# A four-layer decoder trunk on one core: weights split a whole unit at a time, the second keys' strip behind the first, and other room for the inverses

## The chip, the core and the metric

The kernel runs on one core of one Trainium2 chip. TensorE (PE) multiplies matrices, VectorE (DVE) and ScalarE (ACT) do elementwise work and read TensorE's results, GpSimd (POOL) does elementwise work too, and SyncE (SP) issues most of the transfers. The metric is the device time of the whole launch in microseconds; lower is better.

## The reference

Four pre-norm layers act on x, 256 positions of 1024 channels, float32: a pooling mixer, a gated delta net (GDN), a latent attention (MLA), and a pooling mixer again. Each mixer has one input projection, a SiLU gate and one output projection. In the GDN layer, which is where most of this case lies, 8 heads have keys and queries of 128 and values of 256 channels; positions go in chunks of 64:

```python
proj = h @ w_in                       # q, k, v, gate, b, a
qkv = jax.nn.silu(causal_depthwise_conv(qkv, conv_w))     # 4 taps
q, k = l2norm(q) * DK ** -0.5, l2norm(k)
L = where(strict, einsum('bhnid,bhnjd->bhnij', k_beta, k) * decay, 0)
sol = triangular_solve(eye + L, [v_beta, k_beta * exp(g)])
attn = where(causal, einsum('bhnid,bhnjd->bhnij', q, k) * decay, 0)
# then a scan over the chunks with state, w_out behind the gate
```

## The kernel before

**Weights.** Nearly all the work is projections whose weights come from DRAM once. `weights` (L97) loads a unit, two k-blocks of 128 rows by 512 columns (512 KB), by SP into `raw` (three buffers). Each float32 weight is split: ACT casts it into a high part `whi` (L117, fp32r), and DVE subtracts to get the low part `wlo` (L119); for k-blocks listed in `pool`, POOL does the subtraction in DVE's place. The high and low parts lie in the pool `ring`, nine tiles of 512 columns for each. TensorE then does three products in place of one: high by high, low by high and high by low. With `chan=True` (L127 to L129) the channels of the result lie on the partitions, 256 columns (all positions) a product; otherwise (`rows`, L168) positions lie on the partitions and a product has 512 columns. The run of products for one block of 512 output columns is called a strip.

**The GDN layer.** An order is written out by hand in a string of stages, one letter and number each: g a gate's strip, k and q keys and queries (four heads a strip), v a values' strip with its finish, d the decays, a the products `LT` of the keys with each other (`lower`), s the substitution, i the inverses, u the later products. The string before is

```python
order = "g0 k0 d a0 g1 k1 a1 s q0 v0 v1 v2 q1 V3 i c3 g2 u0 u1 g3".split()
```

It sets the order in which the program is written; a scheduler then interleaves the instructions of neighbouring stages on each engine from its own estimates, and decides which buffers share room.

**Around the triangular solve.** `channels` projects, convolves (L637, DVE; the first tap on ACT, L634), applies SiLU into `kqT` (ACT, L671), transposes on TensorE (`tp`, L677) and sums squares (`ssq`, L681). POOL takes the root (`rk`, L659). DVE scales the products of keys into `LT` (L694). `substitution` writes eight 32x32 blocks of `LT` to DRAM (`d_l`, L720, SP) and reads them back laid out by block (`Lb`, L723), then inverts all 64 blocks on POOL in 31 steps of two instructions (`pr`, L728, and `Tb`, L732). POOL sends `Tb` to DRAM (`d_t`, L735) and back into `T` (L739). POOL also multiplies `Gb` with the queries (L760). `inverses` transposes `T` into `U` (DVE, L811), and from the 32x32 inverses builds those of 64x64: `pairs` for both halves of the positions (TensorE, L820 and L826), then `whole` (L834, L838, L844). After them come `u` (L861) and the scan over the chunks (L888 to L914).

**Buffers.** `big` tiles are four KB a partition in a pool whose slots the scheduler hands out. `inverses` has two tiles `X1` of its own among them. The tile `kqT` of the second queries lies where `Lb` was.

## Time and profile before

| | us |
|---|---|
| median of 3 runs | 859.29 |
| lowest and highest run | 856.95, 861.53 |
| the profiled execution | 860.12 |
| its span | 858.3 |
| granted TensorE clock, mean over the span | 0.988 |

In the profile an engine is busy while it carries out instructions; the time that it stands idle is put down to what released it, written behind an arrow. A line number is that of the kernel before. The granted clock is the share of full TensorE speed (2.4 GHz) that the chip allowed; the lower level, 1.2 GHz, reads 0.5. The chain of waits follows the work that ended last back to the start.

### The profile page before, as it was taken

Reading aid. Unit: us, or ns where it says so; the run is one execution under the profiler, and the core shown is the slowest. Engines: PE = TensorE matmul, PEld = TensorE weight load, DVE = VectorE, ACT = ScalarE, POOL = GpSimd, SP = SyncE. Lnnn points to the kernel's source line nnn. Section 1 sums busy time; section 2 is a strip of 40 time slices with the busy share of each in tenths; the row PEclk is TensorE's granted clock in tenths of the full one; section 3 lists DMA queues with packets and bytes.
Section 4 is the critical chain, followed back from the end, with each engine's and each line's share of the span. In section 5 each row is a group of like instructions: output and inputs, shape, how many; then the busy total and the mean of one; then the engine's idle time right before and its main releaser. Section 6 shows DMA issues by size and latency. Waiting matters only on the chain.

```text
span 858.3 us, 16132 instructions
## 1 busy us (share of the span) xinstructions
PE 836.9 (98%) x5967; PEld 778.9 (91%) x5967; DVE 594.2 (69%) x1140; ACT 490.2 (57%) x1007; POOL 155.2 (18%) x295
## 2 busy tenths in 40 slices
PE   6999999999999989999999999999999999999996
PEld 5999998988999988788979998999989989999986
DVE  4689866556988976355577659678767668867852
ACT  5566564467855744355465654566555475555642
POOL 4000000233237980022212002000000210000012
PEclk8999999999999999899999999999999999999999
DMA  6766666646655554123547676743552546556551
GB/s 196 245 190 185 179 194 198 194 138 198 193 141 168 171 149 131 66 67 106 173 139 217 198 171 172 195 127 97 172 163 82 175 148 209 182 179 196 190 201 50
DMA packets 109239, 140.42 MB, mean 164 GB/s; under 512 B 21228, under 2 KB 51112, under 8 KB 109160
## 3 DMA queue, kind: packets, MB, share of 16 engines
q1 hardware_dynamic: 106800, 137.65, 53.1%
q0 software_dynamic: 528, 1.58, 0.7%
q8 instruction: 47, 0.77, 0.4%
q10 hardware_dynamic: 1832, 0.16, 0.2%
q14 instruction: 32, 0.26, 0.1%
HBM read 137.79 MB, written 1.58 MB: 162 GB/s over the span
## 4 chain that ended last, share of the span: by engine, by line
PE 82%; POOL 7%; DVE 5%; DMA 3%; issue 2%; ACT 1%; SPq 0%; POOLq 0%; ACTq 0%; DVEq 0%
PE acc L168 33%; PE acc L128 11%; PE acc L127 11%; PE acc L129 11%; POOL Tb L732 3%; POOL pr L728 2%; PE aux L127 2%; PE aux L128 2%; PE aux L129 2%; DVE wlo L119 1%; DMA gain<-in_norm_g_dram 1%; DVE cv L637 1%; DVE h L304 1%; PE aux L861 1%; DMA Gb<-d_g 1%
## 5 line engine op out<-in xcount | busy, mean ns | idle before, releaser
L119 DVE TENSOR_TENSOR wlo<-raw,whi 128x512 fp32r<-128x512 f32 (+1 forms) x493 | 342.5, 717 | 162.6 <-ACT whi L117 155.4
L117 ACT CAST whi<-raw 128x512 fp32r<-128x512 f32 (+1 forms) x508 | 301.8, 617 | 256.7 <-PE acc L168 100.4
L127 PE MATMUL acc<-hTh,whi 128*128 128x256 f32 x832 | 234.3, 282 | 1.2 <-DVE vc L637 1.2
L128 PE MATMUL acc<-hTl,whi 128*128 128x256 f32 x832 | 235.0, 283 | 0.0
L129 PE MATMUL acc<-hTh,wlo 128*128 128x256 f32 x832 | 233.8, 281 | 0.0
L127 PEld LDWEIGHTS acc<-hTh,whi 128*128 128x128 f32 x832 | 156.9, 189 | 1.8 <-DVE vc L637 1.4
L128 PEld LDWEIGHTS acc<-hTl,whi 128*128 128x128 f32 x832 | 156.9, 189 | 0.4
L129 PEld LDWEIGHTS acc<-hTh,wlo 128*128 128x128 f32 x832 | 156.8, 189 | 0.2
L168 PE MATMUL acc<-wlo,yTh 128*128 128x256 f32 (+1 forms) x384 | 116.5, 319 | 0.0
L168 PE MATMUL acc<-whi,yTh 128*128 128x256 f32 (+1 forms) x384 | 116.4, 323 | 0.0
L168 PE MATMUL acc<-whi,yTl 128*128 128x256 f32 (+1 forms) x384 | 92.7, 322 | 0.0
L168 PEld LDWEIGHTS acc<-wlo,yTh 128*128 128x128 f32 x384 | 72.1, 188 | 5.1
L168 PEld LDWEIGHTS acc<-whi,yTh 128*128 128x128 f32 x384 | 71.7, 188 | 5.2
L168 PEld LDWEIGHTS acc<-whi,yTl 128*128 128x128 f32 x384 | 63.2, 188 | 5.5
L292 POOL TENSOR_TENSOR hg<-x,gain 128x256 f32<-128x256 f32 x18 | 14.9, 834 | 259.1 <-DVE x L354 257.4
L168 PE MATMUL acc<-wlo,hTh 128*128 128x512 f32 (+1 forms) x144 | 56.3, 396 | 0.4 <-DVE wlo L119 0.2
L168 PE MATMUL acc<-whi,hTh 128*128 128x512 f32 (+1 forms) x144 | 55.6, 394 | 0.7 <-ACT hTh L196 0.7
L168 PE MATMUL acc<-whi,hTl 128*128 128x512 f32 (+1 forms) x144 | 45.7, 389 | 0.0
L435 POOL COPY win<-u 128x4 f32<-128x4 f32 x8 | 2.8, 355 | 177.2 <-ACT u L429 177.2
L168 PEld LDWEIGHTS acc<-whi,hTh 128*128 128x128 f32 x144 | 27.5, 191 | 6.8 <-ACT hTh L196 1.7
L168 PEld LDWEIGHTS acc<-wlo,hTh 128*128 128x128 f32 x144 | 27.3, 190 | 6.8 <-DVE wlo L119 1.7
L168 PEld LDWEIGHTS acc<-whi,hTl 128*128 128x128 f32 x144 | 26.8, 190 | 5.5
(339 smaller groups left out, 1444.5 us busy)
## 6 DMA issues: line engine op xcount, KB each, us to landing
raw<-in_pool_w_in_dram SPq DMA_DIRECT2D x60, 512.0 KB, 4.5
raw<-in_gdn_w_in_dram SPq DMA_DIRECT2D x48, 512.0 KB, 3.9
raw<-in_pool_w_out_dram SPq DMA_DIRECT2D x32, 512.0 KB, 4.2
raw<-in_mla_w_in_dram SPq DMA_DIRECT2D x24, 512.0 KB, 4.6
raw<-in_mla_w_uq_dram SPq DMA_DIRECT2D x36, 256.0 KB, 3.4
raw<-in_pool_w_grp_dram SPq DMA_DIRECT2D x16, 512.0 KB, 4.1
raw<-in_gdn_w_out_dram SPq DMA_DIRECT2D x16, 512.0 KB, 3.7
raw<-in_mla_w_ukv_dram SPq DMA_DIRECT2D x32, 256.0 KB, 3.3
```

Of the source, the lines that this page charges most:

```text
L117: a = nc.scalar.copy(hi, v)
L119: b = e.tensor_tensor(out=lo, in0=v, in1=hi.bitcast(F32), op=ALU.subtract)
L127: nc.tensor.matmul(o, lhsT=lhs[0], rhs=rhs[0], start=start, stop=False)
L128: nc.tensor.matmul(o, lhsT=lhs[0], rhs=rhs[1], start=False, stop=False)
L129: return nc.tensor.matmul(o, lhsT=lhs[1], rhs=rhs[0], start=False, stop=stop)
L168: nc.tensor.matmul(o, lhsT=act(k, t * P, P)[x], rhs=parts[j][z][:, sl], start=k == first and x == z == 0, stop=k == last and x == 1)
L292: nc.gpsimd.tensor_tensor(out=self.early[t, a], in0=xs[t][:, sl], in1=self.g[:, sl], op=ALU.mult)
L304: nc.vector.scalar_tensor_tensor(out=h[:, cut:], in0=xs[t][:, sl], scalar=r[:, 0:1], in1=self.g[:, sl], op0=ALU.mult, op1=ALU.mult)
L637: nc.vector.scalar_tensor_tensor(out=o[:, d:], in0=ps[:, :S - d], scalar=tp(3 - d, c), in1=o[:, d:], op0=ALU.mult, op1=ALU.add)
L728: nc.gpsimd.tensor_tensor(out=pv, op=ALU.mult, in0=Lb[:, r, r + 1:, None].to_broadcast([M * Q, n, c]), in1=Tb[:, r:r + 1, :c].to_broadcast ...
L732: mark["blocks"] = nc.gpsimd.tensor_tensor(out=tv, in0=tv, in1=pv, op=ALU.subtract).ins
L861: nc.tensor.matmul(ps[:, c], lhsT=U[0][:, h, :], rhs=vR[h // 2][:, 0, c * DV:(c + 1) * DV], start=True, stop=True)
```

## The change

Three things are changed. In `weights` ACT casts a whole unit, up to 1024 columns, in one instruction, and DVE subtracts a whole unit in one, unless POOL has a part of it (then each k-block has its own subtraction, as before). The ring holds five tiles of 1024 columns in place of nine of 512. Units of one k-block remain 512 wide, and the eight casts of units of 320 columns become four of 640. In all ACT's casts go from 508 to 258 and DVE's subtractions from 493 to 257; TensorE's, POOL's and SP's counts don't change.

In the string of stages the second keys (k1, a1) and the substitution (s) go ahead of the gate's strip g1. The inverses' tiles `X1` are not allocated any more: they are views of `Lb` and `Tb`, whose contents are no longer needed then. Lines move by one to six in the kernel after.

```diff
-    ring = ctx.enter_context(tc.tile_pool(name="ring", bufs=9))
+    ring = ctx.enter_context(tc.tile_pool(name="ring", bufs=5))
...
-        parts = []
-        for k in range(n):
-            v = raw[:, k * cols:(k + 1) * cols]
-            lo = ring.tile([P, CW], F32R, tag="wlo", name="wlo")[:, :cols]
-            hi = ring.tile([P, CW], F32R, tag="whi", name="whi")[:, :cols]
-            held = held_back["free"] <= 0
-            held_back["free"] -= 1
-            with later(*(held_back["after"] if held else ())):
-                a = nc.scalar.copy(hi, v)
+        lo = ring.tile([P, KU * CW], F32R, tag="wlo", name="wlo")
+        hi = ring.tile([P, KU * CW], F32R, tag="whi", name="whi")
+        held = held_back["free"] <= 0
+        held_back["free"] -= n
+        with later(*(held_back["after"] if held else ())):
+            a = nc.scalar.copy(hi[:, :m], raw[:, :m])
+
+            for k in range(n) if pool else (0,):
+                sl = slice(k * cols, (k + 1) * cols) if pool else slice(0, m)
                 e = nc.gpsimd if k in pool else nc.vector
-                b = e.tensor_tensor(out=lo, in0=v, in1=hi.bitcast(F32), op=ALU.subtract)
-            parts.append((hi, lo))
+                b = e.tensor_tensor(out=lo[:, sl], in0=raw[:, sl], in1=hi.bitcast(F32)[:, sl],
+                                    op=ALU.subtract)
+        parts = [tuple(x[:, k * cols:(k + 1) * cols] for x in (hi, lo)) for k in range(n)]
...
-        order = "g0 k0 d a0 g1 k1 a1 s q0 v0 v1 v2 q1 V3 i c3 g2 u0 u1 g3".split()
+        order = "g0 k0 d a0 k1 a1 s g1 q0 v0 v1 v2 q1 V3 i c3 g2 u0 u1 g3".split()
...
-        Tb = big("Tb", B, B)[:M * Q]
+        Tb_ = big("Tb", B, B)
+        Tb = Tb_[:M * Q]
+        free = []
...
-            Lb = big("Lb", B, B)[:M * Q]
+            Lb_ = big("Lb", B, B)
+            Lb = Lb_[:M * Q]
+            free.extend((Lb_, Tb_))
...
-            X1 = [big("X1", H, P) for _ in range(NT)]
+
+            X1 = [a.rearrange("p (h a) c -> p h (a c)", h=H) for a in free]
```

The change moves instructions on the engines. The first place is DVE between the second keys' root and their `LT` products; `s1` and `s2` are the scales that `LT` needs, `cv` the queries' convolution of q0. Before:

```order
294 L705 TENSOR_TENSOR s1_2526<-rk_2522,beta_2466 128x2x4
295 L741 RECIPROCAL rki_2523<-rk_2522 128x16
296 L742 TENSOR_TENSOR kds_2528<-rk_2522,DT_2496 128x8
297 L637 SCALAR_TENSOR_TENSOR cv_3260<-acc_3121,tap_648,cv_3260 128x254
298 L637 SCALAR_TENSOR_TENSOR cv_3272<-acc_3122,tap_648,cv_3272 128x255
299 L707 TENSOR_TENSOR s2_2527<-s1_2526,rk_2522 128x2x4
300 L119 TENSOR_TENSOR wlo_3504<-raw_3498,whi_3505 128x512
301 L637 SCALAR_TENSOR_TENSOR cv_3260<-acc_3121,tap_648,cv_3260 128x253
302 L637 SCALAR_TENSOR_TENSOR cv_3261<-acc_3121,tap_648,cv_3261 128x255
303 L637 SCALAR_TENSOR_TENSOR cv_3272<-acc_3122,tap_648,cv_3272 128x254
304 L694 SCALAR_TENSOR_TENSOR LT_2530<-aux_3017,s2_2527,DT_2496 128x128 x4
305 L694 SCALAR_TENSOR_TENSOR LT_2531<-aux_3026,s2_2527,DT_2497 128x128 x4
```

and after:

```order
226 L119 TENSOR_TENSOR wlo_3139<-raw_3137,whi_3140 128x512
227 L708 TENSOR_TENSOR s1_2304<-rk_2300,beta_2244 128x2x4
228 L746 RECIPROCAL rki_2301<-rk_2300 128x16
229 L747 TENSOR_TENSOR kds_2306<-rk_2300,DT_2274 128x8
230 L710 TENSOR_TENSOR s2_2305<-s1_2304,rk_2300 128x2x4
231 L697 SCALAR_TENSOR_TENSOR LT_2308<-aux_2674,s2_2305,DT_2274 128x128 x4
232 L697 SCALAR_TENSOR_TENSOR LT_2309<-aux_2683,s2_2305,DT_2275 128x128 x4
233 L638 SCALAR_TENSOR_TENSOR cv_2979<-acc_2856,tap_616,cv_2979 128x255
234 L119 TENSOR_TENSOR wlo_3207<-raw_3205,whi_3208 128x1024
```

The convolution of q0 now stands behind `LT`, and one split stands ahead of it.

The second place is DVE behind the last convolution of the second queries (`cv`); `ssq` is their norm, `attnT` their products with the keys, and `U<-T` the transposes that need the inverted blocks back from DRAM. Before:

```order
399 L681 TENSOR_REDUCE ssq_2521<-sq_4010 128x2x2
400 L119 TENSOR_TENSOR wlo_4379<-raw_4373,whi_4380 128x512
401 L119 TENSOR_TENSOR wlo_4397<-raw_4395,whi_4398 128x512
402 L694 SCALAR_TENSOR_TENSOR attnT_3119<-aux_4021,rk_2522,DT_2496 128x128 x4
403 L694 SCALAR_TENSOR_TENSOR attnT_3120<-aux_4030,rk_2522,DT_2497 128x128 x3
404 L681 TENSOR_REDUCE ssq_2521<-sq_4018 128x2x2
405 L694 SCALAR_TENSOR_TENSOR attnT_3120<-aux_4030,rk_2522,DT_2497 128x128
406 L811 STREAM_TRANSPOSE U_4182<-T_2517 128x1024
407 L811 STREAM_TRANSPOSE U_4183<-T_2517 128x1024
```

and after:

```order
315 L119 TENSOR_TENSOR wlo_4009<-raw_4007,whi_4010 128x1024
316 L638 SCALAR_TENSOR_TENSOR cv_3653<-acc_3518,tap_616,cv_3653 128x253
317 L817 STREAM_TRANSPOSE U_3825<-T_2295 128x1024
318 L817 STREAM_TRANSPOSE U_3826<-T_2295 128x1024
319 L684 TENSOR_REDUCE ssq_2299<-sq_3669 128x2x2
320 L119 TENSOR_TENSOR wlo_4027<-raw_4025,whi_4028 128x512
321 L697 SCALAR_TENSOR_TENSOR attnT_2854<-aux_3680,rk_2300,DT_2274 128x128 x4
322 L697 SCALAR_TENSOR_TENSOR attnT_2855<-aux_3689,rk_2300,DT_2275 128x128 x3
323 L684 TENSOR_REDUCE ssq_2299<-sq_3677 128x2x2
324 L697 SCALAR_TENSOR_TENSOR attnT_2855<-aux_3689,rk_2300,DT_2275 128x128
```

The transposes have moved ahead of the norms and the `attnT` products.

The third place is TensorE at the end of the last values' strip (`acc` from `hTh1`, 256 columns) and the first products of the inverses (`aux<-T,LT`); the products of 512 columns are the gate's strip g2. Before, with 13 products of g2 ahead of the inverses' first, of which the last seven are shown:

```order
2130 L168 MATMUL acc_4328<-whi_4332,hTh0_2258 128x512
2131 L168 MATMUL acc_4328<-wlo_4331,hTh0_2258 128x512
2132 L168 MATMUL acc_4328<-whi_4336,hTh0_2258 128x512
2133 L168 MATMUL acc_4328<-wlo_4335,hTh0_2258 128x512
2134 L168 MATMUL acc_4328<-whi_4332,hTl0_2259 128x512
2135 L168 MATMUL acc_4328<-whi_4336,hTl0_2259 128x512
2136 L168 MATMUL acc_4327<-whi_4354,hTh0_2258 128x512
2137 L820 MATMUL aux_4190<-T_2517,LT_2530 128x64 x8
```

and after:

```order
2047 L128 MATMUL acc_3704<-hTh1_2059,whi_3798 128x256
2048 L129 MATMUL acc_3704<-hTl1_2060,whi_3798 128x256
2049 L130 MATMUL acc_3704<-hTh1_2059,wlo_3797 128x256
2050 L826 MATMUL aux_3831<-T_2295,LT_2308 128x64 x8
2051 L169 MATMUL acc_3968<-whi_3973,hTh0_2050 128x512
2052 L169 MATMUL acc_3968<-wlo_3972,hTh0_2050 128x512
```

No product of g2 stands ahead of the inverses' first now.

The order on SP changes at one place: the eight `d_l` transfers, in a row before, go as six, a weight load, and two; between them and `Lb` one weight load stands in both kernels. The tile of the second queries (`kqT`) lies in the room of the first queries' tile after the change, and no longer in that of `Lb`. On POOL a memset and a split that stood between the send of `Tb` and the loads of `T` stand behind the loads.

## Rows read from the trace of the kernel before

**Rows 1.** The page: busy time (share) and instructions by engine; the chain's shares.

```profile
PE 836.9 (98%) x5967; PEld 778.9 (91%) x5967; DVE 594.2 (69%) x1140; ACT 490.2 (57%) x1007; POOL 155.2 (18%) x295
...
PE 82%; POOL 7%; DVE 5%; DMA 3%; issue 2%; ACT 1%; SPq 0%; POOLq 0%; ACTq 0%; DVEq 0%
```

**Rows 2.** Stretches: length, busy time (instructions) by engine, clock, DMA share, GB/s.

```profile
270.00:300.00 30.00, 27.73 (x233) 27.11 (x231) 30.00 (x53) 20.04 (x42) 27.34 (x35) 1.00 0.56 169
300.00:330.00 30.00, 27.59 (x187) 25.21 (x185) 24.93 (x48) 14.13 (x29) 18.70 (x31) 0.94 0.51 144
330.00:360.00 30.00, 28.55 (x175) 23.78 (x175) 11.27 (x18) 11.61 (x23) 1.30 (x1) 0.89 0.32 108
690.00:720.00 30.00, 29.60 (x203) 26.77 (x202) 20.17 (x32) 20.31 (x37) 2.41 (x6) 1.00 0.61 193
```

**Rows 3.** Groups by line and shape: count, busy, mean ns, idle before and its releasers.

```profile
L119 DVE TENSOR_TENSOR wlo<-raw,whi 128x512 fp32r<-128x512 f32 x485 | 338.8, 721 | 160.5 <-ACT whi L117 153.2 <-PE acc L129 2.0 <-PE aux L128 1.5
L117 ACT CAST whi<-raw 128x512 fp32r<-128x512 f32 x500 | 298.3, 620 | 253.9 <-PE acc L168 98.8 <-PE acc L128 79.6 <-DMA raw<-in_pool_w_in_dram 21.1
...
L168 PE MATMUL acc<-wlo,hTh 128*128 128x512 f32 x128 | 51.5, 407 | 0.4 <-DVE wlo L119 0.2
...
L447 DVE TENSOR_TENSOR pl<-p,ph 128x1024 fp32r<-128x1024 f32 x8 | 9.7, 1218 | 0.9 <-ACT ph L446 0.7
...
L446 ACT CAST ph<-p 128x1024 fp32r<-128x1024 f32 x8 | 8.4, 1048 | 1.1 <-DVE p L444 1.1
```

**Rows 4.** The same groups, from 261 to 306 us alone.

```profile
L119 DVE TENSOR_TENSOR wlo<-raw,whi 128x512 fp32r<-128x512 f32 x24 | 22.0, 927 | 2.0 <-PE acc L129 2.0
...
L117 ACT CAST whi<-raw 128x512 fp32r<-128x512 f32 x25 | 14.9, 623 | 9.6 <-DMA raw<-in_gdn_w_in_dram 8.6 <-PE acc L129 0.8 <-PE acc L128 0.2
```

**Rows 5.** Timeline of SP's queue: start, length, line, transfer, count.

```profile
250.69 3.99 SPq L720 DMA_DIRECT2D d_l<-LT  x8
254.78 0.40 SPq L104 DMA_DIRECT2D raw<-in_gdn_w_in_dram  x1
255.93 0.51 SPq L723 DMA_DIRECT2D Lb<-d_l  x1
```

**Rows 6.** Timeline of DVE around the second keys' products.

```profile
245.78 0.85 DVE L637 SCALAR_TENSOR_TENSOR cv<-acc,tap,cv 128x254 f32<-128x254 f32 x2
246.55 1.30 DVE L707 TENSOR_TENSOR s<-s,rk 128x8 f32<-128x8 f32 x1
...
249.55 2.15 DVE L694 SCALAR_TENSOR_TENSOR LT<-aux,s,DT 128x128 f32<-128x128 f32 x8
```

**Rows 7.** Timeline of POOL, the substitution's first and last step and what follows.

```profile
260.95 0.23 POOL L728 TENSOR_TENSOR pr<-Lb,Tb 64x31 f32<-64x31 f32 x1 [13.12 <-DMA Lb<-d_l]
...
305.33 0.25 POOL L732 TENSOR_TENSOR Tb<-Tb,pr 64x31 f32<-64x31 f32 x1
305.54 1.27 POOL L760 TENSOR_TENSOR Gb<-Gb,kqT 128x512 f32<-128x512 f32 x1
```

**Rows 8.** Timeline of ACT, first silu of the second queries; idle before, releaser in brackets.

```profile
305.29 0.42 ACT L671 ACTIVATE kqT<-cv 128x256 f32<-128x256 f32 x1 [3.46 <-POOL pr L728]
```

**Rows 9.** Timeline of TensorE: waits in the layer, and two products of 512 columns.

```profile
277.89 0.65 PE L788 MATMUL tp<-ident,vc 128*128 128x128 f32 x4 [1.11 <-ACT vc L784]
...
305.76 0.69 PE L677 MATMUL tp<-ident,kqT 128*128 128x128 f32 x2 [2.41 <-ACT kqT L671]
...
316.85 0.40 PE L168 MATMUL acc<-wlo,hTh 128*128 128x512 f32 x1
317.08 0.39 PE L168 MATMUL acc<-whi,hTh 128*128 128x512 f32 x1
...
352.91 1.83 PE L844 MATMUL aux<-U,X 64*64 64x64 f32 x16 [0.79 <-DVE X L841]
```

**Rows 10.** Timeline of DVE, products of queries and keys, transposes of the inverted blocks.

```profile
314.10 1.89 DVE L694 SCALAR_TENSOR_TENSOR attnT<-aux,rk,DT 128x128 f32<-128x128 f32 x7
...
318.75 2.37 DVE L811 STREAM_TRANSPOSE U<-T 128x1024 f32<-128x1024 f32 x2 [1.91 <-DMA T<-d_t]
```

## The prediction

> **What bounds the kernel now.** I read the busy times and the chain of waits first. TensorE is busy for 836.9 of 858.3 us and carries 82% of the chain, POOL 7% and DVE 5% [rows 1]. The split of the weights is ACT's and DVE's largest work (298.3 and 338.8 us [rows 3]), but neither engine is the bound over the whole. So the edit is worth what TensorE stands still for, or runs slowly for, and this is read by stretches [rows 2]: nearly full elsewhere (29.60 of 30 us at 690:720, a layer's border), TensorE loses 2.3 us at 270:300, 2.4 at 300:330 and 1.4 at 330:360. There the granted clock falls too, to 0.94 and 0.89: 0.06 x 30 = 1.8 and 0.11 x 30 = 3.3 us of full-clock time, the lower level being 0.5 (1.2 of 2.4 GHz). All three stretches are the gated-delta layer. About 11 us in sum is all that can be had there; the remaining idle time (start, end, borders) is not touched.
>
> Then I read who is waited for. At 270:300 DVE is busy for the whole 30 us: its 24 splits beside POOL's substitution take 927 ns, against 721 over the kernel [rows 3, 4], and TensorE's 1.11 us wait at 277.89 ends with the values' silu behind them. At 300:330 the substitution is the bound. It runs on POOL from 260.95 to 305.58, 44.6 us with hardly a gap [rows 7]; ACT's first silu of the second queries waits 3.46 us for its last `pr`, and TensorE 2.41 us for that silu [rows 8, 9]. What starts it is the DMA of `Lb`, issued at 255.93 behind `d_l` at 250.69 and `LT` at 249.55 [rows 5, 6]. At 330:360 the inverses come with little to put between their dependent steps, and the clock falls before L861.
>
> **The split, a unit at a time.** A unit of 1024 columns cost ACT 2 x 620 = 1240 ns and DVE 2 x 721 = 1442 ns. The same widths as single instructions stand in the trace: ACT's cast of `ph` 1048 ns, DVE's `pl` 1218 ns [rows 3]. So 246 pairs save ACT 0.19 us each, 47 us; 232 pairs save DVE 0.22 us each, 52 us. Elsewhere TensorE is full, so this counts nothing: its cover is TensorE's own strip. It counts at 270:300. About 12 units fall beside the substitution, 12 x 0.22 = 2.7 us off DVE, 12 x (2 x 0.927 - 1.218) = 7.6 us if the collision with POOL cost an instruction and not its columns. I take the lower end, since TensorE's 2.3 us of idle time there is the most that can be gained, and DVE and the raw weights (ACT waited 8.6 us for them [rows 4]) share it. Taken: 1.5 us, bounds 0 and 2.3, and it is lost again if TensorE merely reaches the wait for the second queries sooner.
>
> Against it stands latency: the first half of a unit was ready after 0.620 + 0.721 = 1.34 us, now after 1.048 + 1.218 = 2.27 us, 0.93 later. Five units of look-ahead hide it inside a strip; at the start and three borders the cover is the work ahead of the first strip. Zero taken, bounds 0 and 4 x 0.93 = 3.7 us.
>
> A rule speaks against this edit. The Trainium skill ("Perfetto Trace Analysis", section "Optimizing Scalar/DVE Operations") says that grouping pays where the engine is saturated, but that with unsaturated Scalar or Vector engines that cause bubbles elsewhere "breaking up instructions may allow work to be completed sooner". The trace agrees with the first half at 270:300 alone, where DVE is full; for the rest of the kernel the page's rule is my last rival.
>
> **The second keys' strip behind the first.** On TensorE the gate's strip g1 was ahead of it: 48 matmuls of 512 columns. Such matmuls follow each other by 317.08 - 316.85 = 0.23 us [rows 9], so 11 us. The strip of k1 ends that much sooner. Its transposes do not: in the new order they stand inside g1's strip, and DVE must first finish the decay tiles, the first keys' norm and its own splits. Following the new DVE queue with the durations of before, `LT` of the second keys ends at about 245 to 246, not 251.7. The order shows why: the pieces of q0's convolution and one split that stood between the norm and `LT` are gone, five of the pieces and the split between 245.78 and 249.55 (a piece is 0.85 / 2 = 0.42 us [rows 6]), 2.8 us with the split's 0.7. `d_l`'s eight DMAs now go as 6 and 2 with a weight load between, moving `Lb` by 0.4 us at most (one such issue is 0.40 [rows 5]). So the substitution starts and ends about 6 us sooner, 299.5 instead of 305.5 [rows 7]; bounds 3 (only these pieces gone) and 10 (no new DVE queue in the way).
>
> **What waits for it, and what is new.** Before, the wait of TensorE at 305.76 was 2.4 us [rows 9]. (1) The second queries' tile now lies where POOL's `Gb<-Gb,kqT` reads the first's, so the silu waits for that too: 1.27 us behind the substitution [rows 7]. (2) On POOL a memset and a split between `d_t` and the load of `T` are behind it; by the durations that remain `T` lands some 12 us behind the substitution, 13.2 before (318.75 - 305.54 [rows 7, 10]). (3) On DVE the transposes `U<-T` now stand ahead of the two norms, a split and the `attnT` products. Until `T` lands, DVE does nothing; behind it are 2.37 us of transposes, a norm of about 0.7, a split of 0.7 [rows 3] and the products, 1.89 / 7 = 0.27 us each [rows 10]. TensorE's next strip (g2) needs the bank of the first four: 12 + 2.4 + 0.7 + 0.7 + 4 x 0.27 = 16.9 us behind the substitution. TensorE is there about 2.5 us sooner by the work that is left to it, and stalls so long. Before, 13 matmuls of g2 stood ahead of L820; now none does. (4) Against time from the substitution's end, the second pair's products come at +28.8, before +29.8, but with 15 matmuls of 512 columns less behind TensorE: 15 x 0.23 = 3.5 us. So the net gain is the 6 us, plus 1.0, minus 3.5, minus up to 1.2 us of slow clock behind the stall: 6 - 2.7 = 3.3 at best and 6 - 3.9 = 2.1 at worst. I take 2.7. The 1.5 us of the split are inside it: TensorE's order carries them to the same wait.
>
> **The inverses' own room.** The tiles `Lb` and `Tb` are free by then: no copy, no wait, POOL's memsets move. It removes a slot, nothing on the path. What it lets the order do is put 6 matmuls (1.4 us) between L844 and the products before it; they cover one of the two waits of about 0.8 us that stand before 352.91 [rows 9]. Whether the clock then stays up before L861 is unknown from this trace: it gives 0, or up to 3.3 us [rows 2]. I take 0.5 for the covered wait and 0.8 for the clock, nearer to nothing since one wait of 0.79 remains.
>
> **Sum.** 860.1 (profiled execution) - 2.7 - 0.5 - 0.8 = 856.1, about 4.0 less; the median of the runs is 0.8 below that execution, so 855.3; I say 855.5.
>
> **Rivals.** *Full gain*: the substitution ends 9 to 10 us sooner, the silu and `T` are there when TensorE arrives, and the clock stays up to 360: 10 - 2.7 + 0.5 + 3.3 = 11, 848 us. For it: the strip itself is 11 us earlier. Against: DVE's queue, and TensorE's order that keeps the transposes late. *Hidden anyway*: the chain moves by about 3, new waits take 2.7 to 3.9, the clock falls as before: 859. For it: TensorE is full everywhere else and (1) and (3) are in the order for certain. *DVE stuck behind `T`* (the slower side): the substitution moves by less than 2.7 us, because the second keys' norm waits on DVE behind first keys' work. At an advance of 0, 2.7 to 3.9 us are lost, and a stall of over 4 us takes the clock down for another 1 to 2 us: 863 to 866, say 864.5. It decides below 2.7 us. For it: three waits are now in one chain. Against: q0's pieces are gone for certain. *Breaking up*: whole units make TensorE wait 0.93 us at the start and borders: 855.5 + 3.7 = 859, or 864 if the middle gives little. For it: TensorE idles at these places already; against: its waits for `wlo` in a strip come to 0.4 us in the whole kernel [rows 3].
>
> **How the numbers follow.** Forecast 0.40 (852 to 859), full gain 0.23, hidden 0.20, DVE stuck 0.12, breaking up 0.05. A measurement of this kernel tells about 0.5% from no change, 4.3 us: below 855.0, and above 863.6. Faster: 0.23 and just under half of the forecast, 0.42. Slower: most of DVE stuck and half of breaking up, with some for what I don't see: 0.16. Same: 0.42. The range goes from the full gain, 847.5, to the slower side, 863.5; about 1 in 10 is left out at each end.
>
> **What would show it.** In the new trace: casts near 1048 and 1218 ns; `LT` of the second keys ends near 245.5 and the first `pr` starts near 255; the last `Tb` near 299.5; a silu wait named after `Gb`, not `pr`; `U<-T` with a wait of several us; a stall of TensorE near 316; a clock at 330:360 above 0.89 or not. The forecast is wrong if the substitution's start moves by under 3 or over 9 us, if the splits slow TensorE at borders, or if the clock behind L861 goes another way.

## The result and the profile after

The kernel after takes 863.24 us (median; 861.29 to 865.92), the kernel before 859.70 in the same sessions: ratio 1.0039, 95% interval 1.0025 to 1.0053. It is slower, where about 4 us less were forecast. The profiled execution took 861.29 us, its span 859.5.

The page of after, busy times and the chain's shares, which answer to [rows 1]:

```profile
PE 834.2 (97%) x5967; PEld 780.0 (91%) x5967; DVE 568.4 (66%) x904; ACT 458.0 (53%) x757; POOL 168.5 (20%) x295
...
PE 76%; POOL 7%; DMA 5%; DVE 5%; issue 3%; ACT 2%; SPq 0%; POOLq 0%; ACTq 0%; DVEq 0%
```

DVE and ACT are busy for 26 and 32 us less. TensorE's share of the chain falls from 82 to 76% with the same number of instructions. Stretches of after, columns as in [rows 2]:

```profile
270.00:300.00 30.00, 30.00 (x255) 30.00 (x254) 26.33 (x43) 20.04 (x37) 27.57 (x32) 1.00 0.60 175
300.00:330.00 30.00, 22.75 (x152) 21.09 (x152) 16.30 (x32) 10.16 (x16) 18.26 (x33) 0.83 0.32 90
330.00:360.00 30.00, 28.76 (x183) 23.91 (x183) 13.49 (x17) 11.88 (x18) 1.77 (x1) 0.95 0.48 158
690.00:720.00 30.00, 28.43 (x193) 25.68 (x192) 18.06 (x21) 19.64 (x29) 3.27 (x7) 1.00 0.55 172
```

TensorE's idle time at 270:300 is gone, 2.3 us. At 300:330 it is idle for 7.25 us instead of 2.4, and the clock there is 0.83 instead of 0.94. The splits, over the whole kernel ([rows 3]) and beside the substitution ([rows 4]):

```profile
L119 DVE TENSOR_TENSOR wlo<-raw,whi 128x1024 fp32r<-128x1024 f32 x232 | 290.3, 1255 | 173.4 <-ACT whi L114 172.2
L114 ACT CAST whi<-raw 128x1024 fp32r<-128x1024 f32 x246 | 257.5, 1050 | 236.5 <-PE acc L169 94.0 <-PE acc L129 67.0 <-DMA raw<-in_pool_w_in_dram 26.3
```

```profile
L119 DVE TENSOR_TENSOR wlo<-raw,whi 128x1024 fp32r<-128x1024 f32 x13 | 18.4, 1416 | 2.5 <-ACT whi L114 2.5
```

SP's queue, DVE and POOL, as in [rows 5], [rows 6], [rows 10] and [rows 7]:

```profile
246.62 3.93 SPq L723 DMA_DIRECT2D d_l<-LT  x6
250.65 0.40 SPq L104 DMA_DIRECT2D raw<-in_gdn_w_in_dram  x1
251.09 0.96 SPq L723 DMA_DIRECT2D d_l<-LT  x2
252.15 0.40 SPq L104 DMA_DIRECT2D raw<-in_gdn_w_in_dram  x1
255.35 0.51 SPq L728 DMA_DIRECT2D Lb<-d_l  x1
```

```profile
245.47 2.16 DVE L697 SCALAR_TENSOR_TENSOR LT<-aux,s,DT 128x128 f32<-128x128 f32 x8
...
317.18 2.37 DVE L817 STREAM_TRANSPOSE U<-T 128x1024 f32<-128x1024 f32 x2 [5.02 <-DMA T<-d_t]
```

```profile
258.81 0.23 POOL L733 TENSOR_TENSOR pr<-Lb,Tb 64x31 f32<-64x31 f32 x1 [11.47 <-DMA Lb<-d_l]
...
268.39 1.43 POOL L733 TENSOR_TENSOR pr<-Lb,Tb 64x207 f32<-64x207 f32 x1
269.89 0.60 POOL L737 TENSOR_TENSOR Tb<-Tb,pr 64x207 f32<-64x207 f32 x1
...
305.76 0.24 POOL L737 TENSOR_TENSOR Tb<-Tb,pr 64x31 f32<-64x31 f32 x1
305.97 1.26 POOL L765 TENSOR_TENSOR Gb<-Gb,kqT 128x512 f32<-128x512 f32 x1
```

`LT` of the second keys is done at 247.6, 4.1 us sooner. Nearly all of that is won behind their norm, which comes only 0.4 us sooner: DVE ends its sums of squares (`ssq`) at 241.24, before at 241.68; it starts the scales that `LT` needs 1.6 us sooner. Before, then after:

```profile
241.00 0.68 DVE L681 TENSOR_REDUCE ssq<-sq 128x4 f32<-128x512 f32 x1
245.52 0.15 DVE L705 TENSOR_TENSOR s<-rk,beta 128x8 f32<-128x8 f32 x1
```

```profile
240.57 0.67 DVE L684 TENSOR_REDUCE ssq<-sq 128x4 f32<-128x512 f32 x1
243.92 1.26 DVE L708 TENSOR_TENSOR s<-rk,beta 128x8 f32<-128x8 f32 x1 [1.57 <-POOL rk L662]
```

`Lb` is issued only 0.6 us sooner: the eight `d_l` take 5.4 us to issue instead of 4.0, and `Lb` waits 3.3 us behind the last one (before 1.25). The first `pr` starts 2.1 us sooner (3.5 us behind the issue of `Lb`, before 5.0). But the step of 64x207 at 268.39 takes 1.43 us, its partner 0.60, and the substitution takes 305.76 + 0.24 - 258.81 = 47.2 us instead of 44.6. It ends at 306.0, 0.4 us later than before. ACT and TensorE then read (as [rows 8, 9]):

```profile
307.26 0.42 ACT L674 ACTIVATE kqT<-cv 128x256 f32<-128x256 f32 x1 [10.28 <-POOL Gb L765]
```

```profile
307.73 0.69 PE L680 MATMUL tp<-ident,kqT 128*128 128x128 f32 x2 [7.25 <-ACT kqT L674]
...
355.87 1.14 PE L850 MATMUL aux<-U,X 64*64 64x64 f32 x16 [1.24 <-DVE X L847]
```

TensorE has been waiting since 300.5: it came 3 us sooner, and the silu came 2 us later, 1.26 of them for `Gb`.

By layers, from the start of DVE's last update of x in one layer to that in the next, in us (the first layer's from the start; "again" is a second profile of the same kernel):

| kernel | pooling | GDN | MLA | pooling |
|---|---|---|---|---|
| before | 175.6 | 255.4 | 259.2 | 161.6 |
| before, again | 174.4 | 254.4 | 259.2 | 161.6 |
| after | 174.3 | 257.7 | 258.9 | 161.9 |
| after, again | 174.9 | 258.4 | 258.9 | 161.9 |
| after, borders in halves | 173.1 | 257.2 | 258.4 | 160.8 |
| after, no low parts beside the substitution | 173.7 | 246.8 | 258.8 | 161.8 |
| before, new string alone | 174.6 | 257.6 | 259.3 | 161.7 |

The first column moves by a microsecond between executions of one kernel. What the change adds stands in the GDN layer, 2.3 to 4.0 us; MLA gains 0.3 and the last layer loses 0.3 (by POOL's part of x, which ends later, MLA loses 0.7 and the last layer gains 0.4: the two together stay the same).

### The profile page after: what moved, and what is told of

The parts are those of the page before. It is cut to its first block, busy times and chain, and to the rows that moved or that the text cites. A ratio compares the mean times of both kernels' runs of the same rounds, so it can differ in the third digit from the quotient of the medians.

```text
span 859.5 us, 15387 instructions
## 1 busy us (share of the span) xinstructions
PE 834.2 (97%) x5967; PEld 780.0 (91%) x5967; DVE 568.4 (66%) x904; ACT 458.0 (53%) x757; POOL 168.5 (20%) x295
## 4 chain that ended last, share of the span: by engine, by line
PE 76%; POOL 7%; DMA 5%; DVE 5%; issue 3%; ACT 2%; SPq 0%; POOLq 0%; ACTq 0%; DVEq 0%
PE acc L169 32%; PE acc L130 10%; PE acc L129 10%; PE acc L128 10%; DMA raw<-in_pool_w_in_dram 3%; POOL pr L733 3%; POOL Tb L737 2%; PE aux L128 2%; PE aux L129 2%; PE aux L130 2%; DVE wlo L119 2%; ACT whi L114 1%; DMA raw<-in_mla_w_out_dram 1%; DVE cv L638 1%; PE aux L867 1%
## 5 line engine op out<-in xcount | busy, mean ns | idle before, releaser
L119 DVE TENSOR_TENSOR wlo<-raw,whi 128x1024 fp32r<-128x1024 f32 (+1 forms) x257 | 309.2, 1207 | 191.8 <-ACT whi L114 190.2
L114 ACT CAST whi<-raw 128x1024 fp32r<-128x1024 f32 (+2 forms) x258 | 265.3, 1032 | 245.8 <-PE acc L169 95.0
L129 PEld LDWEIGHTS acc<-hTl,whi 128*128 128x128 f32 x832 | 158.7, 191 | 0.3
L128 PEld LDWEIGHTS acc<-hTh,whi 128*128 128x128 f32 x832 | 158.7, 191 | 0.4
L130 PEld LDWEIGHTS acc<-hTh,wlo 128*128 128x128 f32 x832 | 158.6, 191 | 0.1
L293 POOL TENSOR_TENSOR hg<-x,gain 128x256 f32<-128x256 f32 x18 | 14.7, 829 | 257.1 <-DVE x L355 254.2
L169 PE MATMUL acc<-whi,hTl 128*128 128x512 f32 (+1 forms) x144 | 45.3, 388 | 0.1
L436 POOL COPY win<-u 128x4 f32<-128x4 f32 x8 | 6.1, 765 | 171.8 <-ACT u L430 171.8
```

The costliest lines, as they stand in the source:

```text
L114: a = nc.scalar.copy(hi[:, :m], raw[:, :m])
L119: b = e.tensor_tensor(out=lo[:, sl], in0=raw[:, sl], in1=hi.bitcast(F32)[:, sl], op=ALU.subtract)
L128: nc.tensor.matmul(o, lhsT=lhs[0], rhs=rhs[0], start=start, stop=False)
L129: nc.tensor.matmul(o, lhsT=lhs[0], rhs=rhs[1], start=False, stop=False)
L130: return nc.tensor.matmul(o, lhsT=lhs[1], rhs=rhs[0], start=False, stop=stop)
L169: nc.tensor.matmul(o, lhsT=act(k, t * P, P)[x], rhs=parts[j][z][:, sl], start=k == first and x == z == 0, stop=k == last and x == 1)
```

## The experiments

**The change again, and its parts one by one.** First the same kernel, for a second profile.

> The kernel after once more, for a second profile beside the same kernel before. Theory 1 (three causes in one chain: the transfers d_l land in 3.7 us instead of 1.9, POOL's substitution lasts 47.2 us beside splits of 1024 columns instead of 44.6, and the second queries' silu waits 1.27 us more): LT of the second keys ends about 4 us sooner than before (251.7), the first pr starts only 2 us sooner (about 258.8), the last Tb ends about 306, TensorE waits about 7 us for the silu; the ratio stays near 1.004. Theory 2 (the profile taken first was an accident of the transfers): the first pr starts by 256 or the substitution lasts under 45.5 us here.

Measured 862.26 us, ratio 1.0030 (1.0015 to 1.0046). First `pr` at 260.08, substitution 47.1 us, TensorE's wait 7.8 us. The first start is a microsecond later than expected, as is the whole execution; the rest repeats.

```diff
-    ring = ... bufs=9        # splits of 512 columns
+    ring = ... bufs=5        # weights() of the kernel after, old string, own X1
```

> Before with the splits by whole units and five ring tiles, and nothing else. Theory 1: the substitution lasts 46.5 to 47.5 us (before 44.6), each of its long steps beside a 1024-column split takes up to 1.4 us; the borders of layers lose 1 to 1.5 us each against before, the start gains 1; the time is 861 to 864 us. Theory 2 (the split is neutral and the order carries the loss): substitution 44.5 to 45.5 us, 857 to 860 us.

870.8 us, ratio 1.0123 (1.0092 to 1.0153): worse than either theory. The substitution is only 45.3 us long here, with 9 whole splits beside it, and 9 of its steps are held up. Most of the loss is ahead of it: `LT` ends at 260.2, 8.5 us later than before, though TensorE waits for only 2.8 us in the layer until then; the scheduler's order is another one. Later TensorE waits for the values' convolution and silu:

```profile
PE acc L128 <- DVE vc L638: 4.7, 1, 4.7
PE tp L789 <- ACT vc L785: 2.0, 1, 2.0
```

With the new string and the room as well, a kernel with the same splits is 7 us faster.

```diff
-        order = "g0 k0 d a0 g1 k1 a1 s q0 ...
+        order = "g0 k0 d a0 k1 a1 s g1 q0 ...
```

> Before with the new string of stages and nothing else; splits of 512 columns. The silu of the second queries waits for Gb here too. Theory 1: LT of the second keys ends 4 us sooner, d_l lands later than before (over 2.5 us, before 1.9) because weight loads run beside it, the first pr starts 2 to 3 us sooner, the substitution lasts 44 to 45.5 us, and the time is 856 to 860 us. Theory 2 (the order carries the loss): 862 to 865 us, with a wait of TensorE of over 5 us before the second queries' transposes.

860.5 us, ratio 1.0012 (0.9995 to 1.0029): no change that can be told. `LT` ends at 249.1, but `Lb` is issued at 256.8 and the substitution runs from 260.7 to 306.7. The sooner strip is lost before it reaches POOL. TensorE waits 7.6 us for the silu, as in after, the sign of theory 2, and yet the time is near theory 1's: this wait by itself doesn't make the kernel as slow as after. The substitution is 1.4 us longer than before with the same 24 halves beside it: 6 of its steps are held up by over 0.4 us (before none), 3 of them by 1.0 us, where two halves stand in a row on DVE.

```diff
-            X1 = [big("X1", H, P) for _ in range(NT)]
+            X1 = [a.rearrange("p (h a) c -> p h (a c)", h=H) for a in free]
```

> Before with the inverses in the room of Lb and Tb, and nothing else. The second queries' tile has a room of its own here, so its silu waits for nothing on POOL. Theory 1: the wait of 3.46 us on ACT and of 2.41 us on TensorE at 303 to 306 us is gone, but TensorE then reaches the inverses' first product before T has landed (about 13 us behind the substitution) and gives 1 to 2 us back there: 857 to 859 us. Theory 2 (room counts for nothing): within 0.5 us of before.

863.32 us, ratio 1.0041 (1.0024 to 1.0057), both theories missed. The silu waits for nothing on POOL, as expected, and TensorE runs into the next link:

```profile
PE aux L824 <- DMA T<-d_t: 4.4, 1, 4.4
PE acc L127 <- DVE vc L637: 1.2, 1, 1.2
PE tp L792 <- ACT vc L788: 1.1, 1, 1.1
PE acc L127 <- ACT gsg L557: 1.0, 1, 1.0
```

The wait at the silu, 2.4 us, is traded for one of 4.4 at `T`, and the granted clock at 300:330 is 0.83 here, before 0.94. Giving up two tiles changed the places of others; by the ratios the three parts cost 10.6, 1.0 and 3.5 us and together 3.4, so they don't add up (1.0 is within the spread).

**The wait for the tile.**

```diff
-            dst.append(big("kqT", 4, S))
+            dst.append(own[0] if which and hf else big("kqT", 4, S))   # a const tile
```

> After, with a room of its own for the second queries' tile (one memset more on POOL, long before); the order on every engine is that of after. Theory 1 (the chain from the keys over the substitution to the inverted blocks sets the end, and the wait for the tile only shows where TensorE meets it): the silu no longer waits on POOL, TensorE's stall of 7 us before the second queries' transposes goes, but TensorE then stands at the inverses' first product until T has landed, about 11 us behind the substitution, for 5 us or more; the time falls by 0 to 2 us against after. Theory 2 (the wait for the tile is the loss): the time falls by 5 us or more, to 857 us or below.

862.89 us, ratio 1.0044 (1.0026 to 1.0062), as after. The silu runs at 296.8, TensorE's transposes at 299.6, and then:

```profile
315.17 1.09 PE L828 MATMUL aux<-T,LT 128*128 128x64 f32 x4 [6.92 <-DMA T<-d_t]
```

Theory 1: 7 us of waiting have moved from one place to the next. The tile's room, which I had costed, is not the loss.

**Where the sooner start goes.**

```diff
-                    nc.sync.dma_start(out=lv[t, d],          # and Lb
+                    nc.gpsimd.dma_start(out=lv[t, d],
```

> After, with the transfers of LT to DRAM and back (d_l, Lb) issued by POOL in its own queue and not by SyncE behind and between weight loads. Theory 1 (the 2 us that the earlier keys' strip doesn't bring to the substitution's start are lost in SyncE's queue, where d_l stands between weight loads): d_l lands in 2 to 2.5 us and Lb is issued by 254.5, the first pr starts at 257 to 258.5, in spite of POOL's slower issue (8 x 0.67 us against 3.9). Theory 2 (the transfers are slow because the weight loads use the same DMA engines, whatever the queue): d_l lands in over 3 us here too and the first pr starts no sooner than in after, 258.8 to 260.

862.57 us, ratio 1.0027 (1.0008 to 1.0047). `d_l` lands after 3.7 us (median) here as in after, and `Lb` is issued at 255.5: the queue makes no difference. `Lb` itself took 6.0 us to land and the first `pr` started at 261.6.

```diff
+            if mark.get("hold") and mark["count"] > 0:     # "hold": Lb's transfer, count 6 from v1 on
+                mark["count"] -= 1
+                wait = (mark["hold"],) if mark["count"] < 4 else ()
+            with later(*wait):
                 dma = nc.sync.dma_start(out=dst..., in_=src)   # raw
```

> After, with the third and later weight units of the strip v1 issued by SyncE only behind Lb, so that d_l's eight transfers go in a row and no weight load is issued between them and Lb (they are prefetched some 20 us ahead of TensorE). Theory 1 (d_l lands in 3.7 us and not in 1.9 because weight loads move over the same DMA engines meanwhile; the queue made no difference): d_l lands in 1.8 to 2.5 us, Lb is issued within 2 us of the last d_l (after 3.3), the first pr starts at 255.5 to 257.5 (after 258.8), TensorE's stall of 7 us shrinks by as much and the time falls by 1 to 2.5 us. Theory 2 (d_l is slow by its own small packets): it lands in over 3 us here too, and the time is that of after.

863.13 us, ratio 1.0045 (1.0027 to 1.0063). SP's queue:

```profile
247.37 4.71 SPq L728 DMA_DIRECT2D d_l<-LT  x8
253.35 0.52 SPq L733 DMA_DIRECT2D Lb<-d_l  x1
```

The transfers' size and time to landing (median), and what the DMA engines moved while the last `d_l` were under way (last two numbers: their busy share, GB/s), in before, after and this run:

```profile
d_l<-LT SPq DMA_DIRECT2D x8, 32.0 KB, 1.9
d_l<-LT SPq DMA_DIRECT2D x8, 32.0 KB, 3.7
d_l<-LT SPq DMA_DIRECT2D x8, 32.0 KB, 1.6
```

```profile
252.70:255.70 3.00, 3.00 (x27) 3.00 (x27) 3.00 (x7) 1.58 (x5) 0.00 (x0) 1.00 0.41 63
252.50:255.30 2.80, 2.80 (x26) 2.80 (x25) 2.80 (x7) 0.71 (x2) 0.00 (x0) 1.00 1.00 306
250.00:253.30 3.30, 3.30 (x30) 3.30 (x29) 3.30 (x8) 0.42 (x1) 0.00 (x0) 1.00 0.28 41
```

`Lb` is issued 1.3 us behind the last `d_l`; the first `pr` starts at 257.07. So it is weight loads moving meanwhile that delayed `d_l`. But the time didn't fall: the substitution lasted 50.0 us, with 15 whole splits beside it instead of 13, and ended at 307.0.

**What sets the substitution's length.**

```diff
-            for k in range(n) if pool else (0,):
+            for k in range(n) if pool or mark.get("halves") else (0,):   # in q0, v0, v1, v2, q1
```

> After, with VectorE's splits of the strips q0, v0, v1, v2 and q1 in halves of 512 columns again (ScalarE's casts stay whole). Theory 1 (a subtraction of 1024 columns holds POOL's instruction up for its whole length, some 0.85 us a time): POOL has no or few instructions held up by over 0.4 us (12 in after), the substitution lasts 44.5 to 46 us instead of 47.2, VectorE's own splits beside it take over 0.85 us each. The time falls by 1 to 2 us. Theory 2 (it is the amount, not the width, that slows POOL): the substitution lasts over 46.5 us.

861.82 us, ratio 1.0027 (1.0007 to 1.0048). 45.4 us, 6 steps held up (4 whole splits of other strips remain), end at 303.4. Theory 1 holds in the trace, but the time is not told from after's. TensorE still waits 7.5 us for the silu of the second queries, since on ACT a copy of the values ahead of it now waits for POOL's `Gb`:

```profile
ACT vR L796 <- POOL Gb L765: 10.8, 1, 10.8
```

```diff
-            for k in range(n) if pool else (0,):
+            for k in () if mark.get("nolow") else range(n) if pool else (0,):   # in q0 to V3
...
+        parts = [... for x in (hi, hi if lo is None else lo)) ...]
```

> After, without VectorE's subtractions for the strips q0, v0, v1, v2, q1 and the last values' strip; TensorE's third products of these strips read the high parts in place of the low ones, so that part of the computation is left out and TensorE's work is as before. Theory 1 (VectorE's subtractions beside the substitution hold POOL up, and that is what a sooner start was lost in): no instruction of the substitution is held up by over 0.4 us (12 in after), it lasts 37 to 40 us instead of 47.2 and ends by 299; TensorE's stall before the second queries' transposes shrinks from 7 us to 2 or less, and the time falls by 4 us or more against after, to 858 or below. Theory 2 (the steps are long by themselves or by the other VectorE work): the substitution lasts over 44 us and the time is that of after.

850.61 us, ratio 0.9896 (0.9877 to 0.9915). POOL:

```profile
253.59 0.23 POOL L734 TENSOR_TENSOR pr<-Lb,Tb 64x31 f32<-64x31 f32 x1 [13.42 <-DMA Lb<-d_l]
...
289.93 0.24 POOL L738 TENSOR_TENSOR Tb<-Tb,pr 64x31 f32<-64x31 f32 x1
```

36.6 us, with the same 36 convolutions of values on DVE beside it, and no step held up. This settles what makes the substitution long. Each step's shortest length over all runs, summed, is 31.3 us, and the gaps between steps are 4.8 to 4.9; what is above them is 0.3 us here, 8.5 in before (24 halves) and 10.9 in after (13 whole units). It lies where a split is: in after, 25 of the 62 steps overlap a whole split in time and have 10.8 of the 10.9 us, in before 42 overlap a half and have 8.4 of the 8.5. So a half costs POOL (44.6 - 36.6) / 24 = 0.33 us in before, (46.0 - 36.6) / 24 = 0.39 with the new string alone, and a whole unit (47.2 - 36.6) / 13 = 0.82, more than two halves.

It doesn't settle what the longer substitution costs the kernel. `LT` came at 240.5 here, and four splits of POOL's own in v0, ahead of `LT`, are left out too; so part of the 11 us in the GDN layer is relief of DVE and POOL ahead of the substitution.

**The borders.**

```diff
+            for c in range(n) if fine else (0,):     # first four units of a layer
+                a = nc.scalar.copy(hi[:, cl], raw[:, cl]) ...
```

> After, with the first four units of each layer behind the first one split in halves again, on ScalarE and VectorE. Theory 1 (at a border ScalarE's three whole casts stand ahead of the norm of the second half of the positions, and TensorE's transposes wait for it): the two stretches 174 to 183 and 690 to 697 us are as short as before (7.1 and 6.7 us from the first to the last transposes, after 8.9 and 7.8), and the time falls by 2 to 3 us, to 859.5 to 861. Theory 2 (borders are longer for another reason, the ring of five or raw weights): no change within 0.7 us.

859.09 us, ratio 1.0006 (0.9992 to 1.0020): by the ratios 2.1 to 2.8 us below after, and not told from before, although the substitution is 47.3 us long and TensorE waits 7.1 us for the silu. The time falls as expected, the stretches do not: 8.5 and 7.8 us from the first to the last transposes. By layers it gains 0.5 us in GDN and in MLA and 1.1 in the last one. Why the gain isn't in the stretches where it was expected stays open.

**Combinations, and `T` first.** Three that should have put the pieces together lost.

```diff
-        order = "... s g1 q0 v0 v1 v2 q1 V3 i c3 g2 u0 u1 g3"    # with the own tile
+        order = "... s g1 q0 v0 v1 v2 q1 V3 g2 i c3 u0 u1 g3"
```

> After, with the room of its own for the second queries' tile as in the run before, and the gate's strip g2 ahead of the inverses in the string of stages. Theory 1 (TensorE stands still because all work that needs no inverted block is behind it by then, and what it has left is spent among the inverses' steps): g2's 11 us fill the wait for T (6.9 us with the own tile), but the inverses' steps then have only g3 between them; the stall at T goes, new waits of 2 to 5 us in sum come between 320 and 358, and the clock stays up at 300 to 330; the time falls by 2 to 5 us against after, to 858 to 861. Theory 2 (the inverses' chain needs g2 between its steps and sets the end): the time is within 1 us of after or above it.

864.5 us, ratio 1.0056 (1.0037 to 1.0075). The wait for `T` is gone, but parts of g2's splits are POOL's and queue behind the substitution, which I had not seen:

```profile
PE acc L169 <- POOL wlo L119: 5.1, 1, 5.1
```

> After, with all of it: halves at the borders and beside the substitution, the weight loads held behind Lb, the send of Tb straight behind the substitution's last step, the own tile, g2 ahead of the inverses. Theory 1 (each piece is one link of the same chain or one border): borders give back 3 us, the first pr starts by 257, the substitution lasts 45 to 46 us and ends by 302.5, T lands within 11 us of it, and the time is 852 to 857 us, below both kernels. Theory 2 (the pieces take each other's gain, since TensorE is the bound and only moves its waits): 857 to 861 us.

865.15 us, ratio 1.0055 (1.0032 to 1.0077). The first `pr` is the soonest of these, 256.3, and the substitution the longest, 50.7 us: 10 whole splits of the strips that I had left whole and 13 halves.

> After, with halves at the borders, VectorE's subtractions in halves for the strips q0 to the last values', and the send of Tb and the loads of T ahead of POOL's other work behind the substitution; the second queries' tile has no wait on POOL here. Theory 1 (the end is set by the chain keys, d_l, substitution, T, and by the borders): the substitution lasts 44.5 to 46 us, T lands 9 to 10 us behind it (after 11.2), borders give back 3 us, and the time is 854 to 857.5 us, 2 to 5 us below before. Theory 2 (the chain's links are hidden, TensorE bounds): 858.5 to 860, as with the borders alone.

878.49 us, ratio 1.0217 (1.0193 to 1.0241). The scheduler put the second keys later: `LT` at 255.0, first `pr` at 268.1, and ACT waited 12.3 us for one weight load. It shows no more than that the order decides.

```diff
-                nc.gpsimd.dma_start(out=Ts..., in_=tv[d])       # kernel before
+                mark["blocks"] = nc.gpsimd.dma_start(out=Ts..., in_=tv[d]).ins
...
             with later(mark["blocks"]):         # unchanged: Gb, rq
```

> Before, with the send of Tb and the loads of T ahead of POOL's other work behind the substitution, and nothing else. Theory 1: in before TensorE reaches the inverses' first product just when T lands (318.25 against 318.75), so T sooner by 2 us brings nothing at that place, and the time stays within 1.5 us of before. Theory 2 (T is the link that sets the end there too): 2 us or more below before.

856.98 us, ratio 0.9970 (0.9956 to 0.9983), and once more, with before beside it as a kernel of its own:

> The kernel before itself, for a second profile and for the spread. Both theories: a ratio of 1.000 within 0.002; the layer with the substitution takes 255 to 256 us from the last x of the layer ahead to its own, the substitution 44.5 to 45 us. If the layer's length differs by over 1 us between the two profiles of before, differences of that size between single profiles mean nothing.

> The kernel before with T first, once more. Theory 1 (T sooner has nothing to give, the first ratio of 0.997 was spread): ratio 0.999 to 1.001, the layer 255 to 256 us. Theory 2 (a real gain of the link behind the substitution): ratio 0.996 to 0.998 again, and the inverses' first product on TensorE at 141.5 to 142 us behind the end of the layer ahead (before 142.7).

Before again: 859.13, ratio 0.9997 (0.9979 to 1.0014). T first again: 856.63, ratio 0.9967 (0.9951 to 0.9983). It is 0.3% faster than the kernel before, twice, against theory 1. POOL:

```profile
304.01 0.24 POOL L732 TENSOR_TENSOR Tb<-Tb,pr 64x31 f32<-64x31 f32 x1
304.55 0.64 POOL L735 DMA_DIRECT2D d_t<-Tb  x1 [0.29 <-POOL Tb L732]
305.18 0.34 POOL L810 MEMSET X<- 128x256 f32 x1
307.79 2.00 POOL L739 DMA_DIRECT2D T<-d_t  x3 [2.27 <-DMA d_t<-Tb]
```

The loads of `T` are issued 3.5 us behind the last `Tb`, before 5.9. Yet its two profiles show 255.3 and 257.1 us in the GDN layer, against 255.4 and 254.4, and the inverses' first product comes 141.7 and 143.5 us behind the layer ahead, against 142.7 and 143.5: the gain is in the times and not located in the traces. The two profiles of before differ by 1.0 us in that layer, so a microsecond between single profiles is nothing.

## Why the prediction was wrong

**What bounds the kernel**: right in that the loss stands in the GDN layer, and that less work for ACT and DVE elsewhere moved nothing. The 47 and 52 us were too much: all casts together are busy for 301.8 us before and 265.3 after, all of DVE's splits for 342.5 and 309.2, so 36 and 33 less. The means of the halves had been multiplied by their count, 500 x 0.620 = 310 us on ACT where [rows 3] have 298.3 busy, and 485 x 0.721 = 350 on DVE where they have 338.8.

**The split**: right in its sizes (1050 and 1255 ns against 1048 and 1218) and wrong by what it left out. I priced the split on DVE, where 13 whole ones take 18.4 us beside the substitution and 24 halves 22.0, and never on POOL, though the 927 ns of [rows 4] told that the two engines collide and a collision has two sides. POOL pays 10.6 us for 13 whole units, 8.0 for 24 halves: the substitution is 2.6 us longer. Not all of that is the width, for with the new string alone the same 24 halves cost 9.4. The Trainium skill ("SBUF — State Buffer", section "Who interferes with whom") says that a DVE instruction with two SBUF inputs contends with a GpSimd instruction that reads SBUF, that the ports the two share are an exclusive lock where the order of issue decides who blocks, and that a DVE instruction with at most one SBUF input, outside the 2-port modes, does not contend. The trace agrees: steps beside a whole split take up to 1.0 us more, and with convolutions, which read PSUM, in place of the splits the excess of all 62 steps is 0.3 us. The prediction did not weigh this rule.

**The latency of whole units** at the start and the borders was taken as zero, with bounds of 0 and 3.7 us. Halves there, and nothing else, give back 2.1 to 2.8 us. So this term was mis-sized, and the time fits the rule that it did weigh, breaking up; which wait it is stays open, since the stretches at the borders didn't get shorter.

**The second keys' strip**: the step that failed is "the substitution starts and ends about 6 us sooner". Measured from the end of the layer ahead, `LT` came 3 us sooner, the start 0.9, the end 1.6 later. `LT`: 3 us is the lower bound, for the pieces of q0's convolution that are gone from DVE's queue. The strip's sooner place on TensorE gave nothing more, since the second keys' norm, measured the same way, came 0.8 us later; from 225.7 to 242.3 us DVE is busy without a gap, with the first keys' norm and `LT`, the second keys' convolution and splits. (The stretch of transposes at the border ahead is 1.8 us longer than before, and halves there didn't shorten it; what it has in this is not shown.) `d_l`: "by 0.4 us at most" was for one weight load's issue; eight transfers took 1.4 us longer to issue, and the last landed 2 us later behind its issue because weight loads were moving then (306 GB/s, in before 63). Bounds of 3 to 10 us on one sum, with the length fixed at 44.6, left no room for the case that came.

**The new waits**: the silu behind `Gb` is there (1.26 us), as is DVE's wait for `T`, 5.0 us. TensorE's stall near 316 is not: it was late already, by 7.25 us at the silu. The clock at 300:330 fell to 0.83, as the rival "DVE stuck" had it for a long stall. Before L867 one wait of 1.24 us stayed; the clock at 330:360 is 0.95. Two terms of the prediction rest on no row: "up to 1.2 us of slow clock" and the rival's "1 to 2 us" behind a stall of over 4 us. The runs show 0.11 x 30 = 3.3 us of full-clock time more than before at 300:330 and 0.06 x 30 = 1.8 less at 330:360. And the sum slipped: 1.0 - 3.5 is -2.5, and -3.7 with the clock, where it has 2.7 and 3.9.

**How much of the loss is the substitution's** stays open. With 1.6 us later in the place of 6 sooner, the prediction's terms give 1.6 + 2.5 = 4.1 us of loss, less 0.5 for the covered wait, and the GDN layer lost 2.3 to 4.0. That fits, but it is no test. The string alone has the same stall and the same length of that layer, and its time is 1.0 us above before (-0.4 to 2.5); the substitution 1.8 us shorter (halves beside it), or begun 1.7 us sooner (loads held), changed no time that can be told; and halves at the borders bring the time back to that of before with a substitution of 47.3 us.

**The inverses' room**: "nothing on the path" was wrong in kind: two tiles fewer moved the others, and the run with this part alone is 0.4% slower.

**The rivals**: the slower side came true by its deciding point (the substitution moved by less than 2.7 us), at 863.2 against 864.5; it had 0.12. Its reason, that the second keys' norm waits on DVE, is in the trace and took the first 3 of the 6 us; `d_l` and the substitution's length, which it did not have, took the rest. That its number came so near is in part luck. "Breaking up" is part of the loss too. The time lies at the upper end of the range, 863.5; its sign was missed.

## What to carry to other kernels

When an instruction is made wider on one of two engines that hold each other up, price it on the other one too, above all where that one carries a serial chain: ask what the chain's length would be without the neighbour (here 36.6 us in place of 44.6). A sooner start of a chain is worth what arrives at its end; follow it link by link (transfer, landing, length, next wait), and expect TensorE to wait at the next link by as much. A longer link is not yet the cause of a longer time: mend the link and measure. Parts of a change that a scheduler orders anew don't add up, so each is measured alone and together.

## What the runs showed of the hardware

- A 128x1024 subtraction on DVE with both inputs in SBUF cost POOL's chain 0.82 us (after) to 0.89 ((50.0 - 36.6) / 15, weight loads held), a 128x512 one 0.33 (before) to 0.39 (new string alone); convolutions with an input in PSUM cost it nothing that shows (0.3 us over 62 steps).
- Eight transfers of 32 KB landed in 1.6 to 1.9 us (median) where few or no weight loads moved beside them, in 3.7 with weight loads, from SyncE's queue and from POOL's alike.
- In after TensorE stopped at 300.5 for 7.25 us, and from 302.6 to 312.6 the granted clock was 0.50, the lower level; in before it stopped at 303.4 for 2.4 us, and the clock was 0.50 from 305.4 to 308.6. Over 300:330 this is 0.83 and 0.94; with halves at the borders it is 0.89 with a stall of 7.1 us. Behind the stall matmuls of 256 columns followed each other by 0.21 us for some 5 us, by 0.12 elsewhere.
